# A two-layer attention trunk: the first left operands taken from PSUM, and two products of three panels ahead of the rest

## The chip, the cores and the metric

The kernel runs on one core of a Trainium2 chip. The metric is the device time of one execution in microseconds; the median of several runs counts. TensorE (PE) multiplies, VectorE (DVE), ScalarE (ACT) and GpSimd (POOL) prepare operands and take results away, and SyncE (SP) issues the DMAs. Each engine works through its own instruction list strictly in order, so an instruction that waits holds up everything behind it on the same engine.

## The reference

Cut to what matters here; `x` is 2048 x 1024, `even_w_in` is 1024 x 4100, all float32.

```python
def rmsnorm(x, g):
    y = x * lax.rsqrt(jnp.mean(x * x, axis=-1, keepdims=True) + RMS_EPS)
    return y * g

def even_layer(x, g_norm, w_in, b_f, g_q, g_k, w_out):
    h = rmsnorm(x, g_norm)
    proj = h @ w_in
    fq, fk, fv, f_logit, sq, sk, sv, gate = jnp.split(proj, split_points(EVEN_SIZES), axis=-1)
    ...   # fox attention on f*, stick-breaking attention on s*
    mixed = jnp.concatenate([fox, sb], axis=-1) * jax.nn.silu(gate)
    return x + mixed @ w_out

# odd_layer: rmsnorm, one projection, three dilated window attentions, gate, projection, residual
```

The change touches the first step alone: `rmsnorm` of the first 1024 rows of `x` and their product with `w_in`.

## The kernel before

**The projection.** `even_projection` does two rounds of 1024 token rows. In a round it goes through eight panels of `w_in` with 512 columns each, in the order sq, sk, sv, fv, fk, fq, g0, g1 (the list `kinds`). A panel is one level of a seven-product scheme in the manner of Strassen and Winograd: the left side (2 x 2 blocks of 512 tokens by 512 features) gives seven left operands, A11, A12, S2, S3, S1, A22, S4; the panel's weights (blocks 11, 12, 21, 22) give seven right operands. Each product multiplies one left operand (512 x 512) with one right operand (512 x 256), and `panel` adds the products to the four result blocks. float32 values are split into a high and a low float32r part (`K.split`: ACT or POOL makes `hi`, DVE or POOL makes `lo = src - hi`), and `K.mm3` multiplies hi·hi, hi·lo and lo·hi at lines 91, 92 and 93. A product is 24 matmuls of 512 columns in the panels of mode "d" (sq, sk, g0, g1) and 48 of 256 columns in mode "t".

**Weights.** `Weights` loads a panel's four raw blocks (`wraw`, four buffers in all), forms the combinations on POOL (line 210) and splits them into `wop` tiles, two halves to a product. There are four `wop` buffers, so the fifth half waits until PE is done with the first. In the list of a panel, the low parts of the second, fourth and sixth operand are POOL's, the others DVE's.

**The first left operands.** For the first round `left_direct` makes them from `x` itself. It loads eight tiles of 128 rows (four in `xa`, four in `xb`), scales each by its rows' reciprocal root (`normalise`: a square with a sum on ACT, a short chain on DVE and ACT, a scaling on DVE at line 130), transposes it by eight matmuls with the identity into two PSUM tiles (line 137), and copies these into `fa` (first 512 tokens) or `fb` (next 512), where the norm's weight `ge` is multiplied in, one value for each partition (line 144 on ACT, line 142 on DVE). From `fa` and `fb` in SBUF it forms and splits the operands: A11 and A12 as each tile of `xa` comes, S2 as each tile of `xb` comes (line 399), then S3, S1, A22, S4. Only when this generator is used up (`for _ in first: pass`) does the program write the first panel. The first panel alone uses the order A11, A12, S2, ... (`FIRST`).

**What sets the order.** The program's text goes to a scheduler that puts each engine's instructions in one fixed list; reads of one PSUM tile by two engines get a wait between them, and a pool's next tile waits for the release of the earlier one. Everything after the projection (attention, second layer) is written behind it and waits for its data. For the second round, `transpose_to` writes the normalised, transposed rows to DRAM during the first round's panels, and `left` reads them.

**ACT's tables.** `K.table` asks for one table set (with exp, ln and others) at the start of the kernel. A function that isn't in the loaded set makes a table load; the gate panels at the end of a round use Silu.

Of the kernel before, what the change touches and what calls it, by code (L numbers as in the profile page):

```python
# [36 lines left out]
class K:  # L37
# [57 lines left out]
    def rstd(self, ss, n, width):  # L95

        nc, sm = self.nc, self.small
        ms = sm.tile([P, n], F32, name="ms", tag=f"ms{n}")
        nc.vector.tensor_scalar(ms, ss, 1.0 / width, EPS, op0=OP.mult, op1=OP.add)
        lg = sm.tile([P, n], F32, name="lg", tag=f"lg{n}")  # L100
        nc.scalar.activation(lg, ms, AF.Ln)
        r = sm.tile([P, n], F32, name="r", tag=f"r{n}")
        nc.scalar.activation(r, lg, AF.Exp, scale=-0.5)
        t = sm.tile([P, n], F32, name="t", tag=f"t{n}")
        nc.vector.tensor_tensor(t, r, r, op=OP.mult)
        nc.vector.tensor_tensor(t, t, ms, op=OP.mult)
        nc.vector.tensor_scalar(t, t, -0.5, 1.5, op0=OP.mult, op1=OP.add)
# [69 lines left out]
class Weights:  # L177


    def __init__(self, k, panels, first=False):  # L180
        self.k, self.ready, self.first = k, [], first
        self.loads = ((w, seg, i, q) for i, (w, seg) in enumerate(panels) for q in ("11", "12", "22", "21"))
        self.raw = {}
        self.loaded = 0
        self.gen = self.prepare(panels)

    def load(self, upto):
        nc = self.k.nc
        while self.loaded < upto:
            self.loaded += 1  # L190
            nxt = next(self.loads, None)
            if nxt is None:
                return
            w, seg, i, q = nxt
            n = sum(c[1] for c in seg[0])
            raw = self.k.raws.tile([P, 4, n], F32, name="wraw", tag="raw")
            rows = slice(0, CH) if q[0] == "1" else slice(CH, D)
            at = 0
            for c0, m in seg[int(q[1]) - 1]:
                nc.sync.dma_start(raw[:, :, at:at + m], w[rows, c0:c0 + m].rearrange("(k p) n -> p k n", p=P))  # L200
                at += m
            self.raw[i, q] = raw

    def prepare(self, panels):
        k, nc = self.k, self.k.nc
        for i, (w, seg) in enumerate(panels):
            n = sum(c[1] for c in seg[0])
            self.load(4 * i + 4)
            b11, b21, b12, b22 = [self.raw.pop((i, q)) for q in ("11", "21", "12", "22")]
# [8 lines left out]
            for j, (src, work) in enumerate(steps[a] for a in (FIRST if self.first and i == 0 else ORDER)):  # L218
                for h in range(2):
# [4 lines left out]
                    k.split(t[:, :, 0], t[:, :, 1], src[:, s], "act", "pool" if j in (1, 3, 5) else "dve")  # L224
# [13 lines left out]

def panel(k, A, W, mode, emit, tick, after=None, n=256, first=False):

# [51 lines left out]
    def kept(name):  # L292
        t = k.w4([P, ng, width], name=name, tag=name)
        return [t[:, g] for g in range(ng)]

    u, u3 = kept("u"), kept("u3")
# [99 lines left out]
def left_direct(k, x, A):  # L396

    nc = k.nc
    tt = lambda o, a, b, op: nc.vector.tensor_tensor(o, a, b, op=op)

    def load(xs, b):
        for t in range(TPC):
            for z in range(2):
                c = slice(z * CH, (z + 1) * CH)
                nc.sync.dma_start(xs[:, t, c], x[(b * TPC + t) * P:(b * TPC + t + 1) * P, c])

    def transposed(xt, F, i, on_dve=()):
        k.transposed(xt, k.ge, lambda z: F[:, z * 4:(z + 1) * 4, i], on_dve=on_dve)

    def put(j, i, src, hi_on="pool"):  # L410
        k.split(A[j][:, :, 0, i], A[j][:, :, 1, i], src, hi_on, "dve")

    xa, xb = (k.big([P, TPC, D], name=n) for n in ("xa", "xb"))
    load(xa, 0)
    yield
    load(xb, 1)
    fb, fa = (k.big([P, KT, CH], name=n) for n in ("fb", "fa"))
    A.extend([None] * 7)
    new = lambda *js: [A.__setitem__(j, k.big([P, 4, 2, CH], F32R, name=f"A{j}")) for j in js]
    new(A11, A12, S2)  # L420
    tiles = [xa[:, t] for t in range(TPC)] + [xb[:, t] for t in range(TPC)]
    k.normalise(tiles[0], "dve")
    for t, xt in enumerate(tiles):
        i = slice(t % TPC * P, (t % TPC + 1) * P)
        if t + 1 < len(tiles):
            k.normalise(tiles[t + 1], "dve")
        if t < TPC:
            transposed(xt, fa, i, (1,))
            put(A11, i, fa[:, :4, i])
            put(A12, i, fa[:, 4:, i])  # L430
            continue
        transposed(xt, fb, i)
        s = k.c2([P, 4, P], name="s2")
        tt(s, fb[:, :4, i], fb[:, 4:, i], OP.add)
        tt(s, s, fa[:, :4, i], OP.subtract)
        put(S2, i, s, "act")
    for j, src in ((S3, fa[:, :4]), (S1, fb[:, :4]), (A22, fb[:, 4:]), (S4, fa[:, 4:])):
        new(j)
        for kk in range(4):
            if j == S3:  # L440
                tt(fa[:, kk], fa[:, kk], fb[:, kk], OP.subtract)
            if j == S1:
                nc.gpsimd.tensor_tensor(fb[:, kk], fb[:, kk], fb[:, 4 + kk], op=OP.add)
            if j == A22:
                nc.gpsimd.tensor_tensor(fa[:, 4 + kk], fa[:, 4 + kk], fb[:, 4 + kk], op=OP.subtract)
            if j == S4:
                nc.gpsimd.tensor_tensor(fa[:, 4 + kk], fa[:, 4 + kk], fa[:, kk], op=OP.add)
            k.split(A[j][:, kk, 0], A[j][:, kk, 1], src[:, kk], "act", "dve")


def constants(k, cp, even_norm, odd_norm, even_b_f, even_q_gain, even_k_gain, odd_q_gain, odd_k_gain):
# [4 lines left out]
    k.ident = cs.tile([P, P], F32, name="ident")  # L456
    nc.vector.tensor_scalar(k.ident, jp, 0.0, None, op0=OP.is_equal)
# [87 lines left out]
def even_projection(k, x, w, first, first_left):  # L545
# [14 lines left out]
    def spare():  # L560
        turn[0] += 1
        return ring[0][:, turn[0] % KT]
# [3 lines left out]
    def qk_fox(dst, gain):  # L566
# [5 lines left out]
        def one(block, half, g, src, rs):  # L572
# [8 lines left out]
            k.split(hl[0], hl[1], pt, scale=gain)  # L581
# [39 lines left out]
    def forget():  # L621
# [28 lines left out]
        ("fk", plain(512), "t", qk_fox(k.fT["k"], k.gk)),  # L650
        ("fq", plain(0), "t", qk_fox(k.fT["q"], k.gq)),
# [3 lines left out]
    W = Weights(k, [(w, seg) for _ in range(2) for _, seg, _, _ in kinds], True)  # L655
    W.ahead(1)
    for _ in first:
        pass
    A = first_left
    tick = Pace()  # L660
    tick.every = 2
    for r in range(2):
        B = []
        nxt = left(k, T, 1, B)
        ring[0] = k.big([P, KT, CH], F32R, name="ring")
        for name, seg, mode, emit in kinds:
# [3 lines left out]
            panel(k, A, W, mode, emit, tick, (lambda j: next(nxt)) if last else None,  # L670
                  258 if name == "fv" else 256, r == 0 and name == "sq")
# [509 lines left out]
def tile_hybrid_trunk(ctx, tc, x, even_norm, even_w_in, even_b_f, even_q_gain, even_k_gain, even_w_out,  # L1181
# [49 lines left out]
```

## Time and profile before

| what | value |
|---|---|
| runs, median (lowest to highest) | 2896.94 us (2895.7 to 2902.72), 3 runs |
| profiled execution: its time, its span | 2898.2 us, 2896.1 us |
| mean granted TensorE clock | 0.975 |
| PE busy over the span | 2693.4 us (93%), 20191 matmuls |
| DVE, ACT, POOL busy | 2107.1, 1650.2, 1281.4 us |
| PE busy in the first 100 us | 58.66 us |
| first product's first matmul | 39.62 us after the span's start |

The span is the time from the first to the last instruction; 2.1 us of the execution's own time lie around it. In the views, a row of a timeline has the start, the duration (of all its instructions if merged), engine, line, operation, out<-in, the count, and in brackets the idle time of the engine before it with what ended it. A row of the waits has the waiting engine and line, what ended the wait, the microseconds in total, how often, and the longest. A row of a stretch has each engine's busy time with its count of instructions. The names `A`, `fa`, `fb`, `xa`, `xb`, `wop`, `wraw`, `u`, `c`, `ps` are the kernel's tiles; `ps` is any PSUM tile.

### The profile page before, as it was taken

Reading aid. Unit: us, or ns where it says so; the run is one execution under the profiler, and the core shown is the slowest. Engines: PE = TensorE matmul, PEld = TensorE weight load, DVE = VectorE, ACT = ScalarE, POOL = GpSimd, SP = SyncE. Lnnn points to the kernel's source line nnn. Section 1 sums busy time; section 2 is a strip of 40 time slices with the busy share of each in tenths; the row PEclk is TensorE's granted clock in tenths of the full one; section 3 lists DMA queues with packets and bytes.
Section 4 is the critical chain, followed back from the end, with each engine's and each line's share of the span. In section 5 each row is a group of like instructions: output and inputs, shape, how many; then the busy total and the mean of one; then the engine's idle time right before and its main releaser. Section 6 shows DMA issues by size and latency. Waiting matters only on the chain.

```text
span 2896.1 us, 56017 instructions
## 1 busy us (share of the span) xinstructions
PE 2693.4 (93%) x20191; PEld 2467.0 (85%) x20191; DVE 2107.1 (73%) x4480; ACT 1650.2 (57%) x3992; POOL 1281.4 (44%) x996
## 2 busy tenths in 40 slices
PE   4999999999999988887887999999989999999998
PEld 3899878998899877776887999999978999999876
DVE  7747785675677799999976966666687586663866
ACT  5446453465566666665455564555565477765642
POOL 5545365434233355555654745343335442422322
PEclk8999999999999999998998999999999999999999
DMA  3556635545544433312567463424533445444665
GB/s 117 168 170 224 197 125 170 168 129 185 159 152 135 137 106 116 110 48 75 177 204 228 147 215 99 145 94 148 163 123 98 139 147 161 139 139 138 217 233 197
DMA packets 388164, 437.39 MB, mean 151 GB/s; under 512 B 31472, under 2 KB 319536, under 8 KB 387888
## 3 DMA queue, kind: packets, MB, share of 16 engines
q1 hardware_dynamic: 387888, 433.83, 46.4%
q8 instruction: 159, 2.61, 0.4%
q14 instruction: 117, 0.96, 0.1%
HBM read 279.16 MB, written 154.57 MB: 150 GB/s over the span
## 4 chain that ended last, share of the span: by engine, by line
PE 61%; DVE 24%; DMA 5%; issue 4%; ACT 4%; POOL 1%; SPq 1%; DVEq 0%; ACTq 0%; POOLq 0%
PE ps L91 16%; PE ps L92 16%; PE ps L93 16%; DVE omb L747 4%; PE ps L783 3%; DVE A L86 2%; DVE wop L86 2%; PE ps L1035 2%; DVE S L86 2%; PE ps L1025 2%; PE ps L1006 2%; PE ps L951 1%; DVE lp L319 1%; DVE pT L86 1%; DVE c L277 1%
## 5 line engine op out<-in xcount | busy, mean ns | idle before, releaser
L210 POOL TENSOR_TENSOR wraw<-wraw 128x512 f32<-128x512 f32 (+1 forms) x320 | 444.4, 1396 | 486.5 <-DVE wop L86 210.8
L81 ACT ACTIVATE wop<-wraw 128x512 fp32r<-128x512 f32 (+1 forms) x560 | 350.6, 630 | 372.0 <-PE ps L93 302.1
L86 POOL TENSOR_TENSOR wop<-wraw,wop 128x512 fp32r<-128x512 f32 (+1 forms) x240 | 328.7, 1372 | 508.7 <-ACT wop L81 490.4
L91 PE MATMUL ps<-wop,S 128*128 128x256 f32 (+1 forms) x1792 | 518.9, 290 | 20.0 <-DVE c L277 10.2
L92 PE MATMUL ps<-wop,S 128*128 128x256 f32 (+1 forms) x1792 | 514.2, 287 | 12.2 <-DVE wop L86 9.4
L92 PE MATMUL ps<-wop,A 128*128 128x256 f32 (+1 forms) x1792 | 512.4, 286 | 6.2 <-DVE wop L86 6.0
L91 PE MATMUL ps<-wop,A 128*128 128x256 f32 (+1 forms) x1792 | 511.8, 286 | 6.8 <-ACT u L282 3.1
L93 PE MATMUL ps<-wop,S 128*128 128x256 f32 (+1 forms) x1792 | 514.8, 288 | 0.0
L93 PE MATMUL ps<-wop,A 128*128 128x256 f32 (+1 forms) x1792 | 509.7, 285 | 0.0
L86 DVE TENSOR_TENSOR wop<-wraw,wop 128x512 fp32r<-128x512 f32 (+1 forms) x320 | 266.8, 835 | 236.1 <-ACT wop L81 234.8
L91 PEld LDWEIGHTS ps<-wop,S 128*128 128x128 f32 x1792 | 343.6, 192 | 25.6 <-ACT wop L81 9.6
L92 PEld LDWEIGHTS ps<-wop,S 128*128 128x128 f32 x1792 | 344.4, 192 | 15.4 <-DVE wop L86 10.3
L91 PEld LDWEIGHTS ps<-wop,A 128*128 128x128 f32 x1792 | 341.8, 191 | 11.3 <-issue 4.0
L92 PEld LDWEIGHTS ps<-wop,A 128*128 128x128 f32 x1792 | 342.5, 191 | 8.7 <-DVE wop L86 7.6
L93 PEld LDWEIGHTS ps<-wop,S 128*128 128x128 f32 x1792 | 344.4, 192 | 3.6 <-issue 2.9
L93 PEld LDWEIGHTS ps<-wop,A 128*128 128x128 f32 x1792 | 342.6, 191 | 1.4 <-issue 0.9
L749 POOL TENSOR_TENSOR rows<-rows,omb 128x511 f32<-128x511 f32 (+3 forms) x160 | 189.9, 1198 | 162.4 <-DVE rows L751 76.5
L81 ACT ACTIVATE pT<-ps 128x512 fp32r<-128x512 f32 (+2 forms) x352 | 166.9, 508 | 137.0 <-PE ps L783 69.2
L277 DVE TENSOR_TENSOR c<-u,ps 128x512 f32<-128x512 f32 (+1 forms) x254 | 165.2, 657 | 98.3 <-PE ps L93 86.6
L747 DVE TENSOR_TENSOR_SCAN omb<-omb 128x512 f32<-128x512 f32 (+3 forms) x160 | 220.0, 1379 | 5.9 <-ACT omb L744 3.4
L86 DVE TENSOR_TENSOR pT<-ps,pT 128x512 fp32r<-128x512 f32 (+2 forms) x352 | 189.3, 560 | 31.2 <-ACT pT L81 30.0
L92 PE MATMUL ps<-pT,vt 128*128 128x256 f32 (+1 forms) x576 | 182.2, 317 | 30.7 <-DVE pT L86 30.5
(216 smaller groups left out, 6619.3 us busy)
## 6 DMA issues: line engine op xcount, KB each, us to landing
wraw<-in_odd_w_in_dram SPq DMA_DIRECT2D x80, 512.0 KB, 3.9
wraw<-in_even_w_in_dram SPq DMA_DIRECT2D x64, 512.0 KB, 4.4
ld<-qk SPq DMA_DIRECT2D x106, 256.0 KB, 3.1
qk<-c SPq DMA_DIRECT2D x96, 256.0 KB, 2.4
lp<-hT SPq DMA_DIRECT2D x60, 256.0 KB, 3.4
uu<-ot SPq DMA_DIRECT2D x96, 132.0 KB, 2.0
fin<-uu SPq DMA_DIRECT2D x16, 792.0 KB, 4.8
hT<-te SPq DMA_DIRECT2D x48, 256.0 KB, 3.9
```

The costliest lines, as they stand in the source:

```text
L81: nc.scalar.activation(hi, src, AF.Copy)
L86: (nc.vector if lo_on == "dve" else nc.gpsimd).tensor_tensor(lo, src, hi.bitcast(F32), op=OP.subtract)
L91: mm(out, a[0], b[0], start=start, stop=False, skip_group_check=more)
L92: mm(out, a[0], b[1], start=False, stop=False, skip_group_check=more)
L93: mm(out, a[1], b[0], start=False, stop=stop, skip_group_check=more)
L210: tt = lambda e, o, x, y, op, s: e.tensor_tensor(o[:, s], x[:, s], y[:, s], op=op)
L277: nc.vector.tensor_tensor(out[g], x[g], y[g], op=OP.add)
L747: nc.vector.tensor_tensor_scan(oo[:, ::-1], oo[:, ::-1], oo[:, ::-1], 1.0 if carry is None else carry, OP.mult, OP.bypass)
L749: nc.gpsimd.tensor_tensor(dst[:, :n - 1], dst[:, :n - 1], o[:, 1:n], op=OP.mult)
L783: nc.tensor.transpose(pt[:, (jx * 2 + i) * P:(jx * 2 + i + 1) * P], rows[:, i, (jj * 2 + jx) * P:(jj * 2 + jx + 1) * P], k.ident)
L1006: nc.tensor.matmul(scores(hp, e), q[pr, za, hp], ring[pr, zb, hp, blocks], start=i == 0, stop=i == 2)
L1025: nc.tensor.transpose(pp[:, i * P:(i + 1) * P], row[:, h // 2, h % 2, b], k.ident)
```

## The change

1. **Norm's weight along the rows.** The weight of the norm is loaded once, the same 1024 values into each of the 128 partitions (`gb`), and multiplied in where a tile of `x` is scaled (one scalar_tensor_tensor on DVE for each tile). `xa` and `xb` are loaded a whole row at a time: eight DMAs, not sixteen. The reciprocal roots are made for two tiles at a time after the first two tiles (`rstd` with `m`).
2. **Left operands from PSUM.** The transposed tiles are read in PSUM: ACT makes `hi` from it, DVE makes `lo` from it, and ACT copies it to `fa` (or the first half to `fb`). For the second 512 tokens DVE forms the sums and differences with one operand in PSUM. A22 is split tile by tile, so only S3, S1 and S4 are left for the end. POOL has no more splits of A11 and A12.
3. **Two products of three panels first.** `panel` becomes a generator, `panel_steps`, which yields after the products A11 and A12. The panels sq, sk and sv are opened in turn: six products, with the rest of `left_direct` (one tile of `xb` at a time, a `Pace` step for each product) written between them; then come their other five products each, in the order S2, S3, S1, A22, S4. `Weights` follows: the blocks 11 and 21 for A11 and A12 of the three panels, then all four blocks of each again for the rest, that is six loads of 512 KB more. The results of the six early products go out by way of four free pieces of `fb`.
4. **Constants later.** `constants` (masks, distances, the small vectors' DMAs) is written after the opened panels; only the identity is made at once.
5. **A table request** (`k.table()`) at the start of the second round.

```diff
+EARLY = FIRST[:2]
 class Weights:
+        rest = tuple(j for j in FIRST if j not in EARLY)
+        self.parts = ([(i, EARLY) for i in range(early)] + [(i, rest) for i in range(early)]
+                      + [(i, ORDER) for i in range(early, len(panels))])
...
-                if j >= 3:
-                    self.load(4 * i + 2 + j)
+                if js == EARLY or j in (S3, S1, A22, S4):
+                    self.load()
 def panel_steps(...):
     copy(u, product(A11, x))
     if first:
         result(0, 0, u, product(A12, fresh()))
+        yield
+        u3 = kept("u3")
         plus(u, u, product(S2, fresh()))
 def left_direct(k, x, gain, A, spare):
-    k.normalise(tiles[0], "dve")
-    for t, xt in enumerate(tiles):
+    load(range(1))
+    gb = k.w4([P, D], name="gb")
+    nc.sync.dma_start(gb, gain.to_broadcast([P, D]))
+    load(range(1, TPC))
...
+        nc.vector.scalar_tensor_tensor(tiles[t], tiles[t], roots[t], gb, op0=OP.mult, op1=OP.mult)
...
+        p0, p1 = transposed(t)
+        if t < TPC:
+            for z, j in enumerate((A11, A12)):
+                put(j, i, (p0, p1)[z])
+                nc.scalar.activation(fa[:, z * 4:(z + 1) * 4, i], (p0, p1)[z], AF.Copy)
+            if t == TPC - 1:
+                yield
+            continue
+        a, s1 = fa[:, :4, i], fb[:, :4, i]
+        nc.scalar.activation(s1, p0, AF.Copy)
+        tt(a, a, p0, sub)
+        s = k.c2([P, 4, P], name="s2")
+        tt(s, p1, a, sub)
+        put(S2, i, s)
+        put(A22, i, p1)
+        tt(s1, p1, s1, plus)
+        tt(fa[:, 4:, i], fa[:, 4:, i], s, sub, nc.gpsimd)
+        yield
 def even_projection(...):
-    for _ in first:
-        pass
+    next(first)
...
+    pace.add(first)
+    opened = [panel_steps(k, A, W, mode, emit, pace, first=tag) for (_, _, mode, emit), tag in zip(kinds, tags)]
+    for p in opened:
+        next(p)
+    late()
+    pace.finish()
...
+        if r == 1:
+            k.table()
...
+            if r == 0 and n < len(opened):
+                next(opened[n], None)
+                continue
```

**How the lists move.** On PE, at the start of the list; `xa` and `xb` are the tiles of `x`, A_169 is the left operand A11 of the first product. Before:

```order
L137 MATMUL ps<-ident,xa 128x128 x32
L137 MATMUL ps<-ident,xb 128x128 x16
L91 MATMUL ps<-A_169,wop 128x512 x2
L92 MATMUL ps<-A_169,wop 128x512
L93 MATMUL ps<-A_169,wop 128x512
```

On PE, at the end of the first product (A_127 is A11) and the start of the second (A_128 is A12). In the changed kernel:

```order
L93 MATMUL ps<-A_127,wop 128x512
L464 MATMUL ps<-ident,xb 128x128 x8
L91 MATMUL ps<-A_128,wop 128x512
L92 MATMUL ps<-A_128,wop 128x512
L93 MATMUL ps<-A_128,wop 128x512
```

Before, the transposes of all of `xa` and half of `xb` stand ahead of the first product; now those of `xa` alone do, and each tile of `xb` has its eight transposes behind one of the first four early products.

On DVE, at the end of S2, whose last low part frees the product S2; A_171 is S2, A_480 is S3, `s` a tile's piece of S2. Before:

```order
L399 TENSOR_TENSOR s_452<-fb 128x512
L399 TENSOR_TENSOR s_452<-s_452,fa 128x512
L399 TENSOR_TENSOR s_475<-fb 128x512
L86 TENSOR_TENSOR A_171<-s_452,A_171 128x4x128
L399 TENSOR_TENSOR s_475<-s_475,fa 128x512
L99 TENSOR_SCALAR ms<-ssx 128x1
L399 TENSOR_TENSOR fa<-fa,fb 128x512 x4
L99 TENSOR_SCALAR ms<-ssx 128x1
L86 TENSOR_TENSOR A_171<-s_475,A_171 128x4x128
L86 TENSOR_TENSOR A_480<-fa,A_480 128x512
```

The same place on DVE in the changed kernel, where A_129 is S2, A_130 is A22, A_592 is S3, `c` an early product's result and `fb` the piece that its split goes to:

```order
L86 TENSOR_TENSOR fb<-c,fb 128x512
L295 TENSOR_TENSOR c<-u,ps 128x512
L86 TENSOR_TENSOR A_129<-s_456,A_129 128x4x128
L86 TENSOR_TENSOR A_130<-ps,A_130 128x4x128
L426 TENSOR_TENSOR fb<-ps,fb 128x4x128
L426 TENSOR_TENSOR fa<-fa,ps 128x4x128
L86 TENSOR_TENSOR fb<-c,fb 128x512
L426 TENSOR_TENSOR s_513<-ps,fa 128x512
L86 TENSOR_TENSOR A_592<-fa,A_592 128x512 x4
L86 TENSOR_TENSOR A_129<-s_513,A_129 128x4x128
```

The last piece of S2 now stands behind results of early products and behind all of S3; of the instructions ahead of it, those that read `ps` take one operand from PSUM. The low part of S2's first weights (a `wop` of line 86) follows ten rows further on, behind masks of `constants`.

On POOL, from its first split on; A_169 and A_170 are A11 and A12. Before:

```order
L83 TENSOR_SCALAR A_169<-fa 128x4x128
L83 TENSOR_SCALAR A_170<-fa 128x4x128
L83 TENSOR_SCALAR A_169<-fa 128x4x128
L210 TENSOR_TENSOR wraw<-wraw 128x512 x2
L83 TENSOR_SCALAR A_169<-fa 128x4x128
```

The same place on POOL in the changed kernel:

```order
L86 TENSOR_TENSOR wop<-wraw,wop 128x2x256 x2
L426 TENSOR_TENSOR fa<-fa,s_314 128x4x128
L86 TENSOR_TENSOR wop<-wraw,wop 128x2x256 x2
L426 TENSOR_TENSOR fa<-fa,s_388 128x4x128
L86 TENSOR_TENSOR wop<-wraw,wop 128x2x256
L426 TENSOR_TENSOR fa<-fa,s_456 128x4x128
L221 TENSOR_TENSOR wraw<-wraw 128x512 x2
L86 TENSOR_TENSOR wop<-wraw,wop 128x2x256
```

POOL's splits of the left operands are gone; its first combination of weights (line 221, for S2) comes behind five low parts of early weights and three pieces of S4.

More of the change, by code (lines that the diff above doesn't have):

```diff
@@ L183, in __init__, with load @@
         self.raw = {}
-        self.loaded = 0
-        self.gen = self.prepare(panels)
-    def load(self, upto):
+        self.gen = self.prepare()
+    def load(self):
         nc = self.k.nc
[L189 to L202, printed above, removed]
@@ L204, in prepare @@
-    def prepare(self, panels):
-        k, nc = self.k, self.k.nc
[L206 to L209, printed above, removed]
+        nxt = next(self.loads, None)
+        if nxt is None:
+            return
+        at, i, q = nxt
+        w, seg = self.panels[i]
+        n = sum(c[1] for c in seg[0])
+        raw = self.raw[at, q] = self.k.raws.tile([P, 4, n], F32, name="wraw", tag="raw")
@@ L217, in prepare @@
             }
-            for j, (src, work) in enumerate(steps[a] for a in (FIRST if self.first and i == 0 else ORDER)):
+            for a, j in enumerate(js):
+                src, work = steps[j]
                 for h in range(2):
@@ L236, in get, with panel, panel_steps @@
         return self.ready.pop(0)
[L239 removed]
+def panel(*args, **kw):
+    for _ in panel_steps(*args, **kw):
+        pass
+def panel_steps(k, A, W, mode, emit, tick, after=None, n=256, first=None):
     nc = k.nc
@@ L415, in left_direct @@
     yield
-    load(xb, 1)
-    fb, fa = (k.big([P, KT, CH], name=n) for n in ("fb", "fa"))
+    load(range(TPC, 2 * TPC))
+    fa, fb = (k.big([P, KT, CH], name=n) for n in ("fa", "fb"))
+    spare.extend(fb[:, j].bitcast(F32R) for j in range(4, KT))
     A.extend([None] * 7)
     new = lambda *js: [A.__setitem__(j, k.big([P, 4, 2, CH], F32R, name=f"A{j}")) for j in js]
-    new(A11, A12, S2)
-    tiles = [xa[:, t] for t in range(TPC)] + [xb[:, t] for t in range(TPC)]
-    k.normalise(tiles[0], "dve")
@@ L423, in left_direct, with squares, scaled @@
-    for t, xt in enumerate(tiles):
+    new(A11, A12, S2, A22)
+    roots = {}
+    def squares(*ts):
+        ss = k.small.tile([P, 8], F32, name="ssx", tag="ss4")
+        for j, t in enumerate(ts):
+            nc.scalar.activation(k.c2([P, D], BF, name="junk"), tiles[t], AF.Square, accum_out=ss[:, j:j + 1])
+        r = k.rstd(ss, 8, D, len(ts))
+        for j, t in enumerate(ts):
+            roots[t] = r[:, j:j + 1]
+    def scaled(t):
+        nc.vector.scalar_tensor_tensor(tiles[t], tiles[t], roots[t], gb, op0=OP.mult, op1=OP.mult)
@@ new lines, in transposed, with put @@
+    def transposed(t):
+        pts = []
+        for z in range(2):
+            pt = k.ps("t" if z else "s")
+            for j in range(4):
+                c = z * 4 + j
+                nc.tensor.transpose(pt[:, j * P:(j + 1) * P], tiles[t][:, c * P:(c + 1) * P], k.ident)
+            pts.append(pt.rearrange("p (a b) -> p a b", a=4))
+        return pts
+    def put(j, i, src):
+        k.split(A[j][:, :, 0, i], A[j][:, :, 1, i], src, "act", "dve")
+    squares(0)
+    ahead = {0: (1,), 1: (2, 3), 3: (4, 5), 5: (6, 7)}
@@ L424, in left_direct @@
+    for t in range(2 * TPC):
+        scaled(t)
+        if t in ahead:
+            squares(*ahead[t])
         i = slice(t % TPC * P, (t % TPC + 1) * P)
-        if t + 1 < len(tiles):
-            k.normalise(tiles[t + 1], "dve")
+        p0, p1 = transposed(t)
         if t < TPC:
-            transposed(xt, fa, i, (1,))
-            put(A11, i, fa[:, :4, i])
-            put(A12, i, fa[:, 4:, i])
+            for z, j in enumerate((A11, A12)):
[3 more added lines that the diff above has]
+                yield
```

108 lines of the change are left out of this document (60 added, 48 removed).

## The prediction

> **What bounds the kernel now.** I read the page first: busy times, slices, the chain that ended last.
>
> ```profile
> PE 2693.4 (93%) x20191; PEld 2467.0 (85%) x20191; DVE 2107.1 (73%) x4480; ACT 1650.2 (57%) x3992; POOL 1281.4 (44%) x996
> PE   4999999999999988887887999999989999999998
> PE 61%; DVE 24%; DMA 5%; issue 4%; ACT 4%; POOL 1%; SPq 1%; DVEq 0%; ACTq 0%; POOLq 0%
> ```
>
> PE is the bound; the one slice in which it is half idle is the first (72 us), where the change is made. So next come stretches of 20 us, then PE's waits in the first 100 us.
>
> ```profile
> 0.00:20.00 20.00, 5.32 (x23) 4.55 (x24) 10.47 (x46) 10.41 (x28) 2.77 (x10) 1.00 0.73 219
> 20.00:40.00 20.00, 6.45 (x28) 5.30 (x27) 19.87 (x33) 9.31 (x29) 17.86 (x14) 1.00 0.47 179
> 40.00:60.00 20.00, 14.33 (x64) 11.54 (x63) 14.19 (x27) 15.12 (x43) 8.91 (x7) 0.92 0.09 27
> 60.00:80.00 20.00, 13.19 (x42) 9.56 (x43) 20.00 (x23) 8.95 (x19) 16.55 (x10) 0.66 0.00 0
> ```
> ```profile
> PE ps L137 <- DVE ms L99: 9.8, 1, 9.8
> PE ps L137 <- issue: 9.3, 1, 9.3
> PE ps L91 <- ACT A L81: 8.7, 2, 8.3
> ```
>
> Columns of a stretch: PE, weight loads, DVE, ACT, POOL, then the clock and DMA. DVE has 19.87 of 20 us from 20 to 40 and all of 60 to 80, and POOL is nearly as full there: PE waits for left operands. The timeline of PE dates it.
>
> ```profile
> 39.62 1.20 PE L91 MATMUL ps<-A,wop 128*128 128x512 f32 x2
> 40.62 0.63 PE L92 MATMUL ps<-A,wop 128*128 128x512 f32 x1
> 41.05 0.63 PE L93 MATMUL ps<-A,wop 128*128 128x512 f32 x1
> 46.60 0.39 PE L93 MATMUL ps<-A,wop 128*128 128x512 f32 x1
> 52.19 0.39 PE L93 MATMUL ps<-A,wop 128*128 128x512 f32 x1
> 52.42 1.91 PE L137 MATMUL ps<-ident,xb 128*128 128x128 f32 x16
> 62.61 1.22 PE L91 MATMUL ps<-A,wop 128*128 128x512 f32 x2 [8.28 <-ACT A L81]
> 69.26 0.79 PE L92 MATMUL ps<-A,wop 128*128 128x512 f32 x1 [3.75 <-DVE A L86]
> 138.19 0.28 PE L91 MATMUL ps<-wop,A 128*128 128x256 f32 x1
> ```
>
> Products start at 39.62, cold (41.05 - 40.62 = 0.43 us for a matmul). The second product's 24 matmuls take 52.19 - 46.60 = 5.59 us: a product's price at full clock. Then PE lacks S2, until 62.61 in part and 69.26 in full. The row at 138.19 is the fifteenth product's first (sv's, 256 columns). Fourteen products are 78.3 us, so the first 138 us are worth as much as a PE that stands still until 138.19 - 78.3 = 59.9 us and then never waits. That 59.9 is what the change can cut.
>
> **The change, part by part.**
>
> *Start to first product.* The tiles and ACT's and DVE's prices:
>
> ```profile
> 6.96 1.06 ACT L126 ACTIVATE junk<-xa 128x1024 bf16<-128x1024 f32 x1 [1.30 <-DMA xa<-in_x_dram]
> 9.83 1.06 ACT L126 ACTIVATE junk<-xa 128x1024 bf16<-128x1024 f32 x1 [0.17 <-DMA xa<-in_x_dram]
> L81 ACT ACTIVATE wop<-wraw 128x512 fp32r<-128x512 f32 x10 | 6.1, 627 | 8.3 <-PE ps L93 7.8 <-DMA wraw<-in_even_w_in_dram 0.5
> L126 ACT ACTIVATION_READ_ACCUMULATOR junk<-xa 128x1 f32 x4 | 0.7, 186 | 0.0
> 9.81 1.97 PE L137 MATMUL ps<-ident,xa 128*128 128x128 f32 x8 [9.81 <-DVE ms L99]
> L277 DVE TENSOR_TENSOR c<-u,ps x20: 669/682/689, 51.2 to 178.3; 128x512 f32<-128x512 f32 x20
> L86 DVE TENSOR_TENSOR A<-fa,A 128x512 fp32r<-128x512 f32 x12 | 13.8, 1160 | 0.0
> L86 DVE TENSOR_TENSOR A<-fb,A 128x512 fp32r<-128x512 f32 x5 | 3.2, 678 | 0.0
> L130 DVE TENSOR_SCALAR xb<-xb,r 128x1024 f32<-128x1024 f32 x4 | 3.4, 855 | 0.0
> ```
>
> A further 512 KB lands every 1.43 us ((9.83 - 6.96)/2), so `gb`, second in the queue, takes the second tile's place (7.0) and the tiles 1 to 3 come at 8.4, 9.8, 11.2. The new scaling has two SBUF operands of 1024; the trace has no such row. Bounds: 0.855, the old scaling, and 2 x 1.16; I take 2 x 0.68 = 1.3, since POOL is idle then. Walking the lists: tile 0 is scaled at 8.3 and transposed at 10.2 (1.97 cold). ACT has four squares (1.25 each with the sum's read), and for each tile two splits and two copies (0.63 each), and four weight splits; tiles 1, 2 and 3 leave PE at 16.3, 23.6 and 25.5. The last low part of A11 (0.68 on DVE) ends at 26.7, and the first product starts there, not at 39.6. It is cold as before: eight matmuls at 0.43, sixteen at 0.23, over at 33.9.
>
> *Six early products.* PE's work is unchanged: 32 transposes of `xb` at 0.12 (1.91/16) stand between them. Product 2 ends at 33.9 + 0.95 + 5.6 = 40.5, product 3 at 47.0. Tile 6 can't be transposed then: its scaling stands on DVE behind product 2's results, pieces of S2 and A22 and two result splits, and ends at 48.6, so PE waits 1.6. Products 4, 5, 6 end at 55.2, 61.7, 67.3. Their weights are early: DVE's and POOL's low parts of them come at least 3 us ahead in this walk.
>
> *S2, the seventh product: the term that decides.* From 40.5 DVE has no gap until it waits about 1 us for product 4's result. Ahead of S2's last piece and of the low part of S2's weights stand 16 operations with PSUM in, 17 with two SBUF operands (two of them scalings), and masks and small ones:
>
> - 16 x 0.68 = 10.9 (the row `c<-u,ps`: 669 to 689, never slowed),
> - 15 x 0.68 + 2 x 1.3 = 12.8 without POOL beside them,
> - some two dozen masks and one-column steps, about 4.5 at 0.18 each (the row of masks below: four in 0.72), and 1 of waiting.
>
> That is 40.5 + 29.2 = 69.7 at best. Beside a busy POOL the second kind costs more: 1.16 in the row `A<-fa,A` against 0.678 in `A<-fb,A`. POOL will be busy about 55% of that time (11 operations of about 1.5 in 29 us; its rows follow further down), against 45 to 90% in the stretches of `A<-fa,A`, so I take 0.28 of the 0.48 for each: 17 x 0.28 = 4.8, of which the waiting swallows some. S2 starts at 74. Bounds: 69.7, and 17 x 1.07 more (1.75 in the slowest row, less 0.68):
>
> ```profile
> 1.70 0.72 DVE L469 TENSOR_SCALAR blocks<-jp 32x32 f32<-32x32 f32 x4
> 58.48 1.75 DVE L86 TENSOR_TENSOR A<-s,A 128x512 fp32r<-128x512 f32 x1
> ```
>
> that is 88. PE has then waited 5 to 7 us and may be cold for seven matmuls: 7 x 0.2 = 1.5.
>
> [...] Here 0.682 from PSUM stands against 0.678 from SBUF, so by the row nothing is lost; if reads from PSUM were dearer by a half, S2 would come at 79 and the gain shrink to 12.
>
> *Gain of the start.* Before, PE is worth a start at 59.9, so its seventh product is at 59.9 + 6 x 5.59 = 93.4. Now it is at 74 + 1.5: **-17.9 us**, bounds -23.7 and -4.
>
> *The rest of the three panels* starts with S2 itself, which needs the blocks 12 and 22 and four POOL combinations.
>
> ```profile
> DMA to landing us min/median/max: 3.5/4.2/6.4
> L210 POOL TENSOR_TENSOR wraw<-wraw 128x512 f32<-128x512 f32 x8 | 11.9, 1491 | 8.7 <-DVE t L107 6.8 <-DVE t L105 2.0
> L86 POOL TENSOR_TENSOR wop<-wraw,wop 128x512 fp32r<-128x512 f32 x4 | 6.4, 1618 | 1.2 <-ACT wop L81 1.2
> ```
>
> Block 22 is asked for when the panel before has its A22 weights split (for sq: sv's A11), about 15 us ahead of S2. It takes 4.2 to land, 3.0 for two combinations and 1.3 for a split: 8.5, some 6 us to spare. POOL has 8 x 1.49 + 4 x 1.62 = 18.4 us of work for five products of 28. The six further loads (3 MB) meet an idle DMA (share 0.09 and 0.00 from 40 to 80). I take +1 for the tightest place (S3's low part behind two combinations of S1), bounds 0 and +8.
>
> *The table request.* In round two every pair of Ln and Exp loads tables:
>
> ```profile
> L103 ACT ACT_TABLE_LOAD x8 | 10.3, 1283 | 0.1
> L101 ACT ACT_TABLE_LOAD x7 | 9.0, 1283 | 0.1
> PE ps L579 <- DVE c L574: 3.2, 3, 1.5
> ```
>
> These 15 and two more go, one comes: 20 us of ACT, but PE waits there only 3.2. In round one the same panels wait as long without any load, so I take -1, bounds -4 and 0.
>
> *Later.* Two operations on constants wait for their DMAs on DVE, ahead of the last piece of A12; that is done at 29 in the walk and wanted at 34.9, so 6 us are spare. At the start of attention some instructions of DVE, ACT and SP change places, none on PE's path that I can name: 0, bounds -3 and +3, about the 4.0 that PE waits there for a row maximum:
>
> ```profile
> PE ps L91 <- DVE m L738: 4.0, 1, 4.0
> ```
>
> **Sum.** -17.9 + 1 - 1 = -17.9 us on the profiled execution's 2898.2: 2880.3. The median of the runs is 1.3 lower, so 2879.
>
> **The rivals.**
>
> 1. *DVE becomes the wall.* If DVE's 17 operations each meet POOL and S2 starts at 83 or later, the start is worth less than 93.4 - 84.5 = 8.9 us, about 0.3% (8.7 us), which is roughly the least that a measurement of this kernel can tell from no change. For it: DVE was full for 40 of the first 80 us. Against: these POOL rows, 19.4 us, leave the stretch, and half of DVE's operands now lie in PSUM.
>
> ```profile
> L443 POOL TENSOR_TENSOR fb<-fb 128x512 f32<-128x512 f32 x4 | 6.8, 1708 | 0.6 <-DVE fa L399 0.6
> L83 POOL TENSOR_SCALAR A<-fa 128x512 fp32r<-128x512 f32 x6 | 6.3, 1060 | 2.5 <-ACT fa L144 1.3 <-DVE fa L142 1.1
> L445 POOL TENSOR_TENSOR fa<-fa,fb 128x512 f32<-128x512 f32 x4 | 6.3, 1596 | 2.1 <-ACT fb L144 2.1
> ```
>
> Time: about 2890. Chance 0.15.
>
> 2. *Slower: the weights of the rest.* If block 22 were asked for only when the fourth raw buffer comes free, behind S4's split, its chain of 8.5 us and S3's low part behind four combinations (6 us) would stand open at sq, sk and sv: 3 x 9 = 27 us, and 2880 + 27 = 2907. It decides from 9 us a panel on. For it: raw buffers stay at four, `wop` buffers too, and S2 has lost the product A11 that stood ahead of it. Against: loads were asked for behind the A22 split before as well. Chance 0.06.
> 3. *It does less than it says:* the first product does not start before 35, since `gb` or ACT's squares hold the tiles, and DVE falls behind with it; S2 at 80, gain 12: 2885. It lies in the forecast's range. Chance 0.2, and 0.59 for the forecast at 2872 to 2884.
>
> **How the numbers follow.** The forecast and rival 3 make it faster by over 0.3%, as does a small part of rival 1: faster 0.79. Most of rival 1 is no difference: 0.14. Rival 2 and a bad exchange at attention: slower 0.07. The range: the best start and the best of the other terms is 2896.9 - 23.7 - 5 = 2868; at the other end rival 1 in its larger part, 2892.
>
> **What would show it.** In the profile after: first product's matmul near 27; six products' worth of matmuls (512 and 256 columns) before 70 with one short wait near 47; DVE without a gap from 40 to 74; PE waiting for DVE at S2; S2's first matmul at 70 to 80; no waits of PE for `wop` in sq's, sk's and sv's rest; one table load between the two gate stages where 15 stood at lines 101 and 103; PE's busy time below the sum only by less cold work. The prediction is wrong if S2 comes after 83, if PE waits for `wop` in each of the three panels, or if the gain of the first 140 us is given back at the start of attention.

## The result, and the profile after

| kernel | runs | median (lowest to highest) |
|---|---|---|
| before | 4 | 2897.57 us (2895.7 to 2902.72) |
| changed | 4 | 2865.69 us (2862.05 to 2871.91) |

The ratio is 0.989, 95% interval 0.9867 to 0.9911: 1.1% faster, where 0.6% was predicted; the time lies 2 us below the predicted range of 2868 to 2892. Beside two later sets of runs of the kernel before, the same changed kernel had 2866.93 us (0.9913, 0.9898 to 0.9928) and 2867.08 us (0.9922, 0.9901 to 0.9943). The profiled execution took 2866.85 us, its span 2865.1.

The page after, busy times and slices of PE, then the first four stretches of 20 us:

```profile
PE 2682.5 (94%) x20191; PEld 2459.2 (86%) x20191; DVE 2111.9 (74%) x4453; ACT 1624.1 (57%) x3938; POOL 1261.3 (44%) x981
PE   6999999999999988888797999999989999999998
```
```profile
0.00:20.00 20.00, 3.93 (x16) 3.13 (x16) 10.88 (x25) 13.14 (x28) 3.32 (x9) 1.00 0.94 333
20.00:40.00 20.00, 19.79 (x92) 16.65 (x93) 15.58 (x27) 14.70 (x32) 3.95 (x3) 1.00 0.40 105
40.00:60.00 20.00, 18.35 (x120) 16.29 (x119) 19.31 (x28) 11.56 (x23) 10.44 (x7) 1.00 0.50 152
60.00:80.00 20.00, 13.93 (x63) 11.10 (x62) 19.91 (x32) 8.38 (x17) 12.82 (x10) 0.74 0.22 77
```

From 20 to 40 PE is busy for 19.79 us where it had 6.45, and POOL for 3.95 where it had 17.86. From 40 on DVE is full (19.31, 19.91), and from 60 to 80 PE has gaps and a clock of 0.74. PE's waits in the first 100 us, and rows of its timeline:

```profile
PE ps L464 <- DVE xa L456: 16.3, 3, 8.4
PE ps L93 <- DVE ms L104: 4.1, 1, 4.1
PE ps L92 <- DVE A L86: 1.9, 1, 1.9
PE ps L464 <- DVE xb L456: 1.7, 1, 1.7
```
```profile
20.21 3.68 PE L464 MATMUL ps<-ident,xa 128*128 128x128 f32 x16 [4.92 <-DVE xa L456]
23.72 1.22 PE L91 MATMUL ps<-A,wop 128*128 128x512 f32 x2
25.13 0.40 PE L93 MATMUL ps<-A,wop 128*128 128x512 f32 x1
...
44.76 1.09 PE L464 MATMUL ps<-ident,xb 128*128 128x128 f32 x8 [1.65 <-DVE xb L456]
...
63.53 0.40 PE L91 MATMUL ps<-A,wop 128*128 128x512 f32 x1
65.88 0.68 PE L92 MATMUL ps<-A,wop 128*128 128x512 f32 x1 [1.95 <-DVE A L86]
71.54 0.80 PE L93 MATMUL ps<-A,wop 128*128 128x512 f32 x1 [4.13 <-DVE ms L104]
75.54 0.63 PE L92 MATMUL ps<-A,wop 128*128 128x512 f32 x1
76.35 0.39 PE L92 MATMUL ps<-A,wop 128*128 128x512 f32 x1
```

The first product starts at 23.72 and is at full clock from its fourth matmul on. Six products follow with one wait of 1.65 us. S2, the seventh, begins at 63.53 but waits first for the low part of its last piece (line 92 is hi·lo), then for the low part of its weights (line 93 is lo·hi), and runs cold until 76. DVE's list says what stood in the way:

```profile
57.27 0.68 DVE L426 TENSOR_TENSOR s<-ps,fa 128x512 f32<-128x512 f32 x1
57.87 6.29 DVE L86 TENSOR_TENSOR A<-fa,A 128x512 fp32r<-128x512 f32 x4
64.08 1.75 DVE L86 TENSOR_TENSOR A<-s,A 128x512 fp32r<-128x512 f32 x1
65.75 1.30 DVE L517 TENSOR_SCALAR identb<-jp 128x128 bf16<-128x128 f32 x1
66.97 1.30 DVE L519 TENSOR_SCALAR after<-jp 128x128 bf16<-128x128 f32 x1
...
70.80 0.68 DVE L86 TENSOR_TENSOR wop<-wraw,wop 128x512 fp32r<-128x512 f32 x1
71.40 0.14 DVE L104 TENSOR_SCALAR ms<-ssx 128x1 f32<-128x1 f32 x1
```

Four low parts of S3, which no product wants before S2 is done, take 6.29 us ahead of S2's last piece; two masks take 1.30 each ahead of the weights. (The wait's releaser is named `ms`, which merely follows; the `wop` row before it is what the matmul reads.)

**Where the time came from.** By their tiles, PE's 20191 matmuls stand in the same order in both kernels but for the first 150 us, six places at 421 and 191 places between 752 and 815, so outside of these the same matmul's start can be compared in two traces. The table gives by how many us it comes earlier than in the first trace of before, at the moments of that trace: behind the fv panel's start (174), at the end of round one (456) and of round two (719), and further on.

| trace | 174 | 456 | 719 | 984 | 1498 | 2246 | 2891 |
|---|---|---|---|---|---|---|---|
| changed | 21.0 | 21.4 | 26.9 | 26.4 | 30.9 | 30.3 | 31.5 |
| changed, second trace | 21.4 | 20.3 | 25.8 | 26.4 | 25.2 | 27.5 | 29.3 |
| changed, third trace | 22.0 | 23.2 | 28.6 | 28.7 | 33.0 | 34.5 | 37.5 |
| before, second trace | 1.4 | 1.4 | 1.2 | 2.4 | 5.2 | 5.8 | 7.5 |

Two steps repeat: 21.0 to 22.0 us in the first panels, and 5.4 to 5.5 us in round two. Behind 719 the kernel before differs from itself by 6 us, and the changed one by as much.

### The profile page after: what moved, and what is told of

It reads as the page before. It is cut to its first block, busy times and chain, and to the rows that moved or that the text cites. A ratio compares the mean times of both kernels' runs of the same rounds, so it can differ in the third digit from the quotient of the medians.

```text
span 2865.1 us, 55933 instructions
## 1 busy us (share of the span) xinstructions
PE 2682.5 (94%) x20191; PEld 2459.2 (86%) x20191; DVE 2111.9 (74%) x4453; ACT 1624.1 (57%) x3938; POOL 1261.3 (44%) x981
## 3 DMA queue, kind: packets, MB, share of 16 engines
q8 instruction: 159, 2.61, 0.4%
## 4 chain that ended last, share of the span: by engine, by line
PE 62%; DVE 23%; DMA 6%; issue 4%; ACT 3%; POOL 1%; SPq 0%; DVEq 0%; ACTq 0%; POOLq 0%
PE ps L91 17%; PE ps L93 17%; PE ps L92 17%; DVE omb L820 5%; PE ps L856 2%; PE ps L1108 2%; DVE A L86 2%; DVE wop L86 2%; PE ps L1098 2%; DVE S L86 2%; PE ps L1079 2%; DVE pT L86 1%; PE ps L1024 1%; DVE lp L340 1%; DMA lp<-hT 1%
## 5 line engine op out<-in xcount | busy, mean ns | idle before, releaser
L91 PEld LDWEIGHTS ps<-wop,S 128*128 128x128 f32 x1792 | 342.1, 191 | 23.6 <-DVE c L295 8.3
L92 PEld LDWEIGHTS ps<-wop,S 128*128 128x128 f32 x1792 | 342.9, 191 | 16.9 <-DVE wop L86 11.6
```

Source lines behind the costliest of these rows:

```text
L91: mm(out, a[0], b[0], start=start, stop=False, skip_group_check=more)
L92: mm(out, a[0], b[1], start=False, stop=False, skip_group_check=more)
```

## The experiments

Each lead below is against the first trace of the kernel before, as in the table.

**The table request: taken out of the changed kernel, and put alone into the kernel before.**

```diff
-        if r == 1:
-            k.table()
```

> The changed kernel without the table request ahead of the second round; nothing else differs. Theory A (the request is worth 5 us, not the 1 us of the prediction): in the kernel before TensorE waits 3.2 us for the normed rows in fk and fq of round two and 0.9 us in the forget gate, beside 15 table loads of 1.28 us, and in the changed kernel none of these waits is left; so without the request the loads come back, the same waits come back, the lead over the kernel before falls from 21.4 us at the end of round one to 21 to 22 us behind fq of round two instead of 26.9, and the time is 2866 + 5 = about 2871 us. Theory B (the prediction's: the waits have another cause, the loads lie beside other work): the waits stay away or come in either kernel, and the time is 2866 + 1 = 2867 us at most.

> The kernel before with the table request ahead of the second round and nothing else of the change. Theory A: one load stands where 15 stood, the 4.1 us of waits in the second round go, and the time is 2897.5 - 5 = about 2892.5 us. Theory B: the 15 loads go, the waits stay, 2896.5 us.

Without the request: 2874.46 us (5 runs), ratio to before 0.9937 (0.9923 to 0.995), that is 7.5 us over the changed kernel's 2866.93 beside it. Alone: 2886.07 against 2892.36, 0.9977 (0.9966 to 0.9988). From 456 to 719 the first loses 0.4 us of lead (23.8 to 23.4) where the changed kernel gains 5.4 to 5.5, and the second gains 5.4 (1.8 to 7.2). PE's wait and ACT's loads in round two, without the request:

```profile
PE ps L637 <- DVE c L632: 3.6, 4, 1.6
L108 ACT ACT_TABLE_LOAD x8 | 10.3, 1283 | 0.1
L106 ACT ACT_TABLE_LOAD x7 | 9.0, 1283 | 0.1
```

With the request alone PE has no such wait there. Theory A holds: it is worth 5.4 us, not 1. What the loads do shows in the kernel before, in ACT's and DVE's timelines of a normed panel of round two:

```profile
604.25 1.28 ACT L101 ACT_TABLE_LOAD   x1
605.77 1.28 ACT L103 ACT_TABLE_LOAD   x1
607.06 0.21 ACT L103 ACTIVATE r<-lg 128x8 f32<-128x8 f32 x1
607.30 0.17 DVE L105 TENSOR_TENSOR t<-r 128x8 f32<-128x8 f32 x1 [2.25 <-ACT r L103]
```

Both loads lie between `ms` and `r`, on the chain from a result to its transposition, and DVE stands for 2.25 us. PE does not wait at that place. In round two it waits at four others: for the forget gate's `ya` (0.95 us) and for `c` at 624.13 (1.54), 643.42 (0.87) and 670.73 (0.78). The first of them, with its two loads:

```profile
572.21 1.28 ACT L627 ACT_TABLE_LOAD   x1
573.78 1.28 ACT L628 ACT_TABLE_LOAD   x1
575.64 0.33 PE L632 MATMUL ps<-ident,ya 128*128 128x128 f32 x1 [0.95 <-DVE ya L630]
```

At these four places the lead grows, by 1.2, 2.1, 1.1 and 1.2 us, alike in the changed kernel and in the kernel with the request alone. That is all of the 5.4 us, though the waits themselves come to 4.1.

In round one, where no load is, the same wait of PE has another cause, seen on DVE in the changed kernel while POOL works:

```profile
243.48 1.26 DVE L114 TENSOR_TENSOR r<-r,t 128x8 f32<-128x8 f32 x1
244.77 3.44 DVE L632 TENSOR_TENSOR c<-c,r 128x512 f32<-128x512 f32 x2
248.13 1.23 DVE L111 TENSOR_TENSOR t<-t,ms 128x8 f32<-128x8 f32 x1
```

The two scalings take 1.72 each, not 0.65 (1.29 for two a little later), and steps on eight columns 1.2, not 0.17.

**One panel opened, and two.**

```diff
-    W = Weights(k, [...], 3)
-    tags = ("u", "x", "x")
+    W = Weights(k, [...], 1)
+    tags = ("u",)
```

> The changed kernel with only the first panel opened ahead: two products before the transposes of the second four tiles instead of six. Parts one and two of the change (first left operands from PSUM, weight along the rows) stay. Theory A (the start's gain is TensorE work brought into a stretch that VectorE sets): the first product still comes near 23.7 us; the third left operand's chain on VectorE loses some 10 us of work for the opened panels and its product starts near 61 us instead of 63.5 with waits up to 71.5, but four products of 5.6 us (22.4 us) are still to come then, so the time is 12 to 15 us longer than the changed kernel: about 2879 us. Theory B (the gain came from the earlier first product, and the opened panels only put work before the same VectorE wall): at most 4 us longer, 2866 to 2870 us.

> The changed kernel with two panels opened instead of three. One panel alone led the kernel before by 9.2 us at the fv panel of round one, three by 21.0. Theory A (the seventh product's wall on VectorE stays near 62 to 65 without the third panel's work, and products are worth their 5.6 us up to there): the second panel brings nearly its full 11.2 us and the third only the rest, so the lead at fv is 18 to 20 us, and the changed kernel loses 1 to 3 us by it. Theory B (each panel is worth the same): a lead of 15 us at fv, 6 us lost. The order of TensorE's list near the end of the program may differ as it does in the kernel with one panel, so the lead at fv is what tells, not the whole time.

One panel: 2890.54 us, 0.9994 of before (0.9985 to 1.0003). Two: 2871.65 us, 0.992 (0.9906 to 0.9934). Leads at 174: 9.2 and 17.2. With one panel PE and DVE from 40 to 60, and PE's two waits there:

```profile
40.00:60.00 20.00, 3.65 (x17) 3.35 (x17) 19.84 (x34) 6.77 (x13) 11.80 (x9) 0.59 0.30 100
```
```profile
50.53 3.58 PE L464 MATMUL ps<-ident,xb 128*128 128x128 f32 x16 [13.17 <-DVE xb L456]
59.93 1.65 PE L91 MATMUL ps<-A,wop 128*128 128x512 f32 x3 [5.82 <-ACT A L81]
```

PE has 3.65 us of work beside a full DVE; S2 starts at 59.93, 3.6 earlier than with three panels, but with four products (22.4 us) still to do. So all of the change but the second and third panel is worth 9 us of the start (parts 1, 2 and 4 and the opening of one panel were not taken apart); the second panel brings 8.0 more and the third 3.8. With one panel the start loses 11.8 us, about the 12 of theory A and far from theory B's 4. With two, the second panel brings more than the third, as theory A has it, but the lead of 17.2 lies between its 18 to 20 and theory B's 15. (One panel's 2890.54 is 23.6 us more than the changed kernel beside it, which the start does not explain: the lead is 16.3 at 719 and 14.9 at 2740, and falls to 7.2 by 2880, a stretch in which this kernel's list for PE stands in another order. That order was not studied.)

**The first left operands from SBUF again.**

```diff
-                put(j, i, (p0, p1)[z])
                 nc.scalar.activation(fa[:, z * 4:(z + 1) * 4, i], (p0, p1)[z], AF.Copy)
+                put(j, i, fa[:, z * 4:(z + 1) * 4, i])
```

> The changed kernel with the first two left operands split from the copy of the transposed tile in SBUF instead of from PSUM (part one of the change undone for them). Theory A (reading PSUM spares a ScalarE copy on the path and keeps VectorE's lows at 0.68 us): the first product comes 0.6 us later, the eight lows take up to 1.7 us beside GpSimd instead of 0.68, tiles 5 to 7 come later by some of that; 2 to 5 us longer, about 2870 us. Theory B (VectorE is no wall before 40): 0.6 us, no measurable difference, 2867 us.

2874.45 us, 0.9937 of before (0.9923 to 0.9951); the lead at 174 is 16.3 us, 4.7 to 5.7 less. PE's timeline at the first product, and DVE's there:

```profile
25.33 1.22 PE L91 MATMUL ps<-A,wop 128*128 128x512 f32 x2 [1.60 <-ACT A L81]
28.92 0.79 PE L92 MATMUL ps<-A,wop 128*128 128x512 f32 x1 [2.37 <-DVE A L86]
```
```profile
23.21 0.69 DVE L86 TENSOR_TENSOR A<-fa,A 128x512 fp32r<-128x512 f32 x1 [0.82 <-ACT A L81]
26.98 0.23 DVE L545 SCALAR_TENSOR_TENSOR oq<-oq,ok 128x64 f32<-128x64 f32 x1 [3.01 <-DMA ok<-in_odd_k_gain_dram]
28.18 0.69 DVE L86 TENSOR_TENSOR A<-fa,A 128x512 fp32r<-128x512 f32 x1
```

The loss at 174 is about theory A's upper end but not by its reason: the lows take 0.69 as ever (POOL is nearly idle from 20 to 40, 0.80 us). PE waits 1.60 for ACT's split, ahead of which ACT's copies now stand, and 2.37 for a low part of A11, since these have slid behind an operation that waits 3.01 us for the small vector `ok`; then its matmuls run cold, 0.43 apart, up to 32. The first product ends 5.7 us later. In the changed kernel the same operation waits 2.61, but the lows of A11 are done ahead of it. So the run shows what the way by SBUF costs in this order, about 5 us of the start (the medians are 7.5 us apart, but stem from different sets, and the intervals of the ratios overlap); what it costs without that transfer, 1.6 or somewhat more, was not tried. The Trainium skill (VectorE: DVE Perf Modes, "Rules for kernel authors") advises the copy where many operations follow on a matmul's output; here two splits follow, and to copy ahead of them was the dearer way.

**What stands ahead of S2 on DVE.** Masks at the start; S3's, S1's and S4's splits made to read a value from S2's last piece (`one`, always 1), so that the scheduler can't put them ahead of it; the two operations on the small gains read it too:

```diff
+        if t == 2 * TPC - 1:
+            nc.vector.tensor_scalar(k.one, A[S2][:, 0, 1, CH - 1:].bitcast(F32), 0.0, 1.0, op0=OP.mult, op1=OP.add)
...
-            k.split(A[j][:, kk, 0], A[j][:, kk, 1], src[:, kk], "act", "dve")
+            nc.scalar.activation(A[j][:, kk, 0], src[:, kk], AF.Copy, scale=k.one)
+            nc.vector.tensor_tensor(A[j][:, kk, 1], src[:, kk], A[j][:, kk, 0].bitcast(F32), op=sub)
```

> The changed kernel with VectorE's list altered around the seventh product: the masks (identb, after, notbefore, blocks, dist) are made at the start, behind ident, where VectorE waits for the first tile; the small gains' two operations and the four splits of the third sum (S3) read a value that the last piece of S2 makes, so they come behind that piece. In the changed kernel S2's last low part ends at 65.8 (behind four lows of S3, 6.29 us) and the lows of its weights at 71.5 (behind 2.6 us of masks and more), its product waits 0.7 + 0.8 rows with 1.9 and 4.1 us ahead and TensorE runs at half clock to 76. VectorE also waited 2.6 us for a small transfer at 24.5 to 27.1. Theory A (VectorE's order at 58 to 71 is what now sets the start of S2, and the half clock follows from its gaps): S2 runs through from 63.5 without a wait over 1 us, and the time falls by 6 of waits and up to 5 of clock, less what S3 loses: by 8 us (4 to 11), about 2859 us. Theory B (the total of VectorE's work to S3 and S1 is the wall, in whatever order): the wait only goes to S3 or S1, and the time stays within 2 us of 2867.

2865.29 us, 0.99 (0.9885 to 0.9915): no difference from the changed kernel that the runs can tell, and a lead at 174 of 23.1, one to two more. S2 ran through from 63.6 without a wait, but the wait came back one product later, for PSUM:

```profile
72.39 0.47 PE L91 MATMUL ps<-A,wop 128*128 128x512 f32 x1 [3.04 <-DVE c L295]
74.10 0.80 PE L91 MATMUL ps<-A,wop 128*128 128x512 f32 x1 [1.00 <-DVE c L295]
```

The sixth product's results lay in two of the four banks, and DVE took them out at 71.57 and 73.37, behind S3's low parts. By itself that speaks for theory B. The next kernel tells B from a wrong order: `one` is read from the sixth product's result, so that DVE empties the banks first (and the small vectors' DMAs and the small gains come behind all splits).

```diff
-            nc.vector.tensor_scalar(k.one, A[S2][:, 0, 1, CH - 1:].bitcast(F32), 0.0, 1.0, ...)
+            nc.vector.tensor_scalar(k.one, cs[1][:, 0:1], 0.0, 1.0, op0=OP.mult, op1=OP.add)
```

> As the run with the masks at the start, but the splits of the third, fifth and last left operands (S3, S1, S4) read a value made from the sixth product's result, so that VectorE takes that result out of PSUM before them; the small gains come behind all splits. There TensorE waited 3.0 and 1.0 us at 72.4 and 74.1 for PSUM banks that VectorE had not emptied (rows of c from u and ps at 71.6 and 73.4, behind four lows of S3). Theory A (what TensorE waits for is which row VectorE takes first): no such wait, the next product follows S2 near 69.2 with waits of about 1 us, the lead at fv rises from 23 to 27 us, the time is about 2861 us (2858 to 2864). Theory B (VectorE's total up to the eighth and ninth product is the wall, whatever comes first): the wait goes to another row, the lead at fv stays within 1 us of 23, about 2865 us.

2858.23 us (2857.31 to 2861.68), 0.989 of before (0.9874 to 0.9906), beside 2867.08 and 0.9922 (0.9901 to 0.9943) for the changed kernel in the same set: the fastest of all. The lead is 27.6 at 174 and 28.6 at 456 (21.0 to 22.0 and 20.3 to 23.2 in the changed kernel): about 6 us of the start by the traces, 9 by the medians. PE and DVE from 60 to 80, and the waits left in the first 160 us besides those for the tiles:

```profile
60.00:80.00 20.00, 17.78 (x88) 14.10 (x87) 19.95 (x30) 14.17 (x26) 12.47 (x8) 1.00 0.34 110
PE ps L93 <- DVE wop L86: 1.3, 1, 1.3
PE ps L92 <- DVE t L112: 0.8, 1, 0.8
```

DVE is as full as before (19.95), PE has 17.78 us where it had 13.93, at full clock. Theory A: it was the order of DVE's work, not its sum. (The masks left this stretch too, but with them and the first gate alone the lead grew by one to two.)

**Four panels**, plain (with `constants` ahead of the fourth), and with the masks at the start and the small gains late:

```diff
-    tags = ("u", "x", "x")
+    tags = ("u", "x", "x", "x")
```

> The changed kernel with four panels opened ahead (fv too), and the small constants ahead of the fourth since fv needs one of them. Lead at fv over the kernel before with one, two, three panels: 9.2, 17.2, 21.0 us. Theory A (TensorE's products fill the time up to VectorE's wall, which the fourth panel's own rows on VectorE, some 8 us, push back): the eighth product ends near 74.8 and S2 follows at 75 to 78, which is worth a seventh product at 64 to 67 against 72.5 now: 5 us faster (0 to 8), a lead behind fv of about 26 us and 2862 us. Theory B (VectorE is full from 40 on, so what the fourth panel adds there is paid later, as PSUM waits of the products behind S2): within 2 us of 2867.

> Four panels opened, the masks at the start where VectorE waits for the first tile, and the two operations on the small gains behind all splits (in the changed kernel VectorE waits 2.6 us for one of them at 24.5). Theory A: 2 us less than four panels alone, as the masks alone gave 2 us with three panels: about 2860 us. Theory B: VectorE is no longer what TensorE waits for with four panels, and it is the same within 1 us.

> The changed kernel as it is, beside the three others of this call: 2866 us, and a third trace whose lead over the kernel before is 20 to 21.5 us at fv and 25.5 to 27 us at the 700th us, and differs from the others by some us behind that.

2873.98 us (0.9944, 0.9929 to 0.9959) and 2872.76 us (0.9933, 0.9916 to 0.995), beside 2867.08 with three panels: the plain one is 7 us slower, for the other the intervals overlap. Neither theory foresaw where the loss comes. S2 follows at 76.9, as theory A said. But fv's two products now run before the job that transposes round two's rows is started, so that job reaches into the panel fq (its last copy starts at 287.2, in the changed kernel at 236.5), where ACT does its copies ahead of the norm's squares:

```profile
PE ps L637 <- DVE c L632: 11.5, 4, 8.6
```
```profile
285.41 2.17 ACT L149 ACTIVATE te<-ps,ge 128x128 f32<-128x128 f32 x8
287.42 1.20 ACT L123 ACTIVATE sq<-c 128x512 f32<-128x512 f32 x2
...
291.69 0.63 ACT L123 ACTIVATE sq<-c 128x512 f32<-128x512 f32 x1 [2.04 <-DMA hT<-te]
```

One wait of 8.6 us (9.5 in the second kernel), and the lead at 456 is 15.7 and 21.7. That reading is from the trace; the job's start was not moved to test it. Whether the masks alone are worth something with four panels is open (intervals overlap).

**The changed kernel again** (2866.93 us) served for the second trace, the third came with the run above; the kernel before was traced again too:

> The changed kernel as it is, for a second trace. The first trace leads the kernel before by 26 us where attention starts and by 31.5 us at the end, though the instructions of TensorE stand in the same order there. Theory A (the 4.6 us are variation from run to run): the second trace differs from the first by up to a few us in the attention and the lead at the end is anywhere from 27 to 34 us. Theory B (they belong to the change): it repeats to within 1 us, growth of 4 to 6 us between the 1040th and the 1300th us.

> The kernel before as it is, for a second trace. If the 4 to 6 us of difference in the attention between the first two traces are variation, this trace differs from the first of the same kernel by as much there, and by under 1 us up to the 720th us.

The table shows the outcome: theory A. The sizes expected were too narrow: the third trace, expected at 20 to 21.5 and 25.5 to 27, leads by 22.0 at 174 and 28.6 at 719, and the second trace of before is 1.2 to 1.4 us off already in the first 720 us. The 4.6 us that the first pair of traces grows apart behind 719 are within what one kernel differs from itself.

## Where the prediction held, and where it failed

The time was to be 2879, in a range of 2868 to 2892, and was 2865.7, below the range. The mechanism held; the steps that failed are the sizes of three terms: the start, the table request, and what comes later. The sum said -17.9. The profiled executions differ by 31.35 and the medians by 31.9, but beside the two later sets of the kernel before by 25.4 and 24.2, so 6 to 8 us of the 31.9 are not shown to belong to the change. (The low end of the range was added up wrongly too: it takes 5 us for the best of the other terms, whose bounds, 0, -4 and -3, make 7. That gives 2866, still above what was measured.)

- **Start to first product: 26.7 predicted, 23.72 measured.** The failed step is the walk's "tiles 1, 2 and 3 leave PE at 16.3, 23.6 and 25.5": tiles 2 and 3 were transposed together from 20.21 to 23.6. "It is cold as before" failed with it. Those sixteen transposes had PE busy for 3.5 us, and matmuls came 0.23 apart from the fourth on. In the kernel with two panels, whose list is the same up to there, the first two matmuls already took 0.73 us, not 1.22, so the transposes alone can bring the clock up. The Trainium skill (TensorE: Matmul & The Clock Gate, Part 1) gives a window of about 3.4 us of work; here the fourth matmul comes 4.9 us after the first of the transposes, which fits, but no run measures the window.
- **Six early products** went as walked: the wait for tile 6 was 1.65 (1.6 said), the sixth product ended at 63.5 (67.3 less the 3 above and the cold matmuls).
- **S2.** DVE's way from the second product's end to S2 was 33.5 us in the walk (40.5 to 74) and 35.0 in the trace (36.5 to 71.54): the sum held, but it began 4 us earlier. That it held is in part luck. Masks "at 0.18 each" took 1.30 beside POOL, and S3's four lows 1.57 each; the operations with two SBUF operands came to 20 us where 17.6 stood, the small ones to 6.0 where 4.5 stood. Against that, neighbouring rows start 0.60 apart where 0.68 was counted for each (57.27 and 57.87 above). And the walk took S2 to stand still until all its parts were there, where four of its matmuls ran before 67.5; its cold stretch, up to 76, was about twice the seven matmuls said.
- **Gain of the start with the rest of the panels: -16.9 said, 21.0 to 22.0 measured** (1.4 less against the second trace of before): 4 us mis-sized. PE had no wait for `wop` in the rest of sq, sk and sv up to 140, so the +1 for it was 0.
- **The table request: -1 said, 5.4 measured**, outside the bounds of -4 and 0. The failed step is "in round one the same panels wait as long without any load", taken to mean that the loads cost nothing. The waits are alike in size and differ in cause, as the rows at 244 and 604 show; two experiments put the loads' share at 5.4 us, at PE's four waits of round two, of which the prediction had counted three.
- **Later: 0 said, 4.6 us gained in the first pair of traces,** of which nothing is shown to belong to the change. The bounds of 3 were taken from one wait of PE; the same kernel's traces differ by 6 us there. PE's own list changes between 752 and 815, which the prediction did not name, but the lead is as large behind it as ahead (26.4 and 26.9). With 4.1 of the start, 0.4 in the rest of round one and 4.5 of the request this makes about the 13.4 us between the sum and the profiled execution.
- **The rivals.** Rival 1 (DVE as the wall) is half true: S2's last wait ended at 71.5, not behind 83, yet DVE's order still costs about 6 us of the start. Rival 2 (weights) and rival 3 (a late first product) did not come. Of the chances, "faster" (0.79) came; the time fell outside the forecast's 2872 to 2884 (0.59).

## What to carry to other kernels

Where a full engine feeds TensorE, count not only its sum but which row it takes first: a scheduler that takes what is ready put four splits and a few masks ahead of the one piece that TensorE wanted, and an order that gives TensorE its piece, and its PSUM banks, first was worth 6 us of the start (9 by the medians) with the engine just as full. Two waits of equal size in two stages may have different causes, so before a cost is struck out by analogy, look at the chain behind each wait. Work brought forward pays only up to the next wall and then collides with what it passed: the second panel brought 8.0 us, the third 3.8, and the fourth lost 7, by the trace to a job that slid into a stage that had no room for it.

## What was not expected of the hardware

In proportion, small operations on DVE lose most beside POOL: a 128x128 mask with one SBUF operand took 1.30 us where it takes 0.21, and steps on one or eight columns 1.20 to 1.26 where they take 0.15 to 0.17. They last until POOL's operation ends: the two masks of 1.30 end at 67.05 and 68.27, and these POOL rows of the changed kernel at 66.96 and 68.19.

```profile
63.62 3.34 POOL L221 TENSOR_TENSOR wraw<-wraw 128x512 f32<-128x512 f32 x2
66.93 1.26 POOL L86 TENSOR_TENSOR wop<-wraw,wop 128x512 fp32r<-128x512 f32 x1
```

The same mask in the kernel with one panel, with POOL idle:

```profile
53.31 0.21 DVE L517 TENSOR_SCALAR identb<-jp 128x128 bf16<-128x128 f32 x1
```

The Trainium skill (SBUF — State Buffer, "Who interferes with whom") counts a `tensor_scalar` in a two-port mode among the operations that POOL blocks, for the whole of an instruction; these rows agree, though no run shows in which mode the masks ran. The 128x512 float32 sums and differences with one PSUM operand took 0.64 to 0.70 us in every trace, beside POOL or not.
